# q and k of the first mixer in one pass over the feature blocks of a decoder layer, v behind them

## The chip, the cores and the metric

One core of a Trainium2 chip runs one decoder layer with float32 inputs. The metric is the device time of one execution in microseconds, as the median of three runs. TensorE (PE) multiplies, VectorE (DVE) and ScalarE (ACT) work on elements, GpSimd (POOL) takes a few subtractions and powers, and SyncE (SP) issues transfers.

## The reference

x is (1, 512, 1024), c is (1, 1024). All of it is computed in float32.

```python
mod = silu(c) @ ada_w + ada_b
shift1, scale1, gate1, shift2, scale2, gate2 = split(mod, 6)
h = rmsnorm(x, norm1_g) * (1 + scale1) + shift1
qa, ka, va, qb, kb, vb, ga, gb = split(h @ w_in)      # 512, 128, 128, 3 x 512, 2 x 1024 columns
ya = swa_attention(qa, ka, va, sinks, rel_bias) @ w_branch_a     # 8 q heads, 2 kv heads, window 128
yb = moba_attention(qb, kb, vb, rel_bias) @ w_branch_b           # 8 heads, blocks of 256
x = x + gate1 * ((sigmoid(ga) * ya + sigmoid(gb) * yb) @ w_out)
h2 = rmsnorm(x, norm2_g) * (1 + scale2) + shift2
x = x + gate2 * (square(relu(h2 @ w_mlp_in)) @ w_mlp_out)
return rmsnorm(x, final_g)
```

## The kernel before

The 512 tokens are four tiles of 128, the 1024 features are eight blocks of 128. Each float32 factor of a product is split in a rounded part (ScalarE, `split` line 71) and the rest (VectorE, line 72), and each product is issued three times (`mm3`, lines 76 to 78): high by high, high by low, low by high.

The change touches the first stage, from the loads to the start of the attention heads. It needs, for each block f of features, the columns shift1 and 1 + scale1. `ada_first` (line 266) loads the modulation weights of a block, 8 x 256 columns, blocks 0 and 1 together and the others singly. `columns` multiplies each of the eight row groups by silu(c) and adds them up, the first on ScalarE (line 292), seven on VectorE (line 294), in a PSUM bank that each group has for itself (`pac`); the last sum goes to SBUF (`acc`). TensorE then adds over the partitions with a column of ones (line 299), and `finish_cols` adds bias and 1 and multiplies by the gain in three small VectorE steps (lines 168 to 170). `normed` takes the mean square of a token tile on ScalarE (line 122), its power -1/2 on GpSimd (line 126) and scales x (line 309). `features` transposes block f of the scaled tiles to `px` (line 313), `modulated` scales and shifts it (line 317) and splits it to `hT` (lines 71 and 72), and `project` multiplies it with the 512 q columns of `w_in` into four banks `g0p` that stay open over all eight blocks: 4 x 3 products for a block. `g0_split` splits the q weights (ScalarE line 281, GpSimd line 282). Block 0 is done in two halves of two tiles.

Behind the loop k and v of the first mixer are multiplied from one load `kvr`: 24 products each, of 512 columns (`pkv`). `stack_q` and `stack_k` split the results and copy them to the other half of the partitions; all four q pairs are emitted ahead of the heads. Then `run` emits 16 heads, each with scores, softmax, transposes and values, and between them pieces of dense products as the table `PACE` says. The first dense pieces are `proj_v` (`pv`).

What sets the order: the program is written out in one order and a planner orders each engine's queue by a simulation. Within the first stage the queues of TensorE and SyncE follow the written order (`manual_schedule`), with later products put in between where the planner sees room; the other engines follow the planner. A tile of a pool waits for the buffer that it takes over, and PSUM has eight banks, all from one pool. SyncE has eight transfers under way at most: each issue takes over the semaphore of an older one.

Of the kernel before, what the change touches and what calls it, by code (L numbers as in the profile page):

```python
# [15 lines left out]
P = 128  # L16
# [21 lines left out]
def decoder_layer(ctx: ExitStack, tc: tile.TileContext, x, c, ada_w, ada_b, norm1_g, norm2_g, w_in,  # L38
# [63 lines left out]
    for g in range(2):  # L102
        V.tensor_scalar(swap[g], ident, 0.0, None, op0=ALU.mult)
        A.activation(swap[g][:, 64 * g:64 * g + 64], ident[:, 64 - 64 * g:128 - 64 * g], AF.Copy)
# [105 lines left out]
    with ExitStack() as sa:  # L210
# [30 lines left out]
        with ExitStack() as ss:  # L241
# [10 lines left out]
            n_ada = 0  # L252

            def ada_first(fs):

                nonlocal n_ada
                w, tiles, nk = len(fs) * P, [], KT // len(fs)
                for i in range(len(fs)):
                    name, n_ada = f"ad{n_ada}", n_ada + 1
                    n = n_ada - 1  # L260
                    t = (p0.tile([P, 2048], F32, name=name, tag=("at0h", "at0l", "at1h", "at1l")[n % 7])
                         if n % 7 < 4 else raw(name))
                    t = t.rearrange("p (k s n) -> p k s n", k=nk, s=2)
                    for s in range(2):
                        c0 = s * D + fs[0] * P
                        SY.dma_start(t[:, :, s], wk[:, i * nk:(i + 1) * nk, c0:c0 + w])
                    tiles.append(t)
                ads[fs[0]] = lambda k: tiles[k // nk][:, k % nk]

            def g0_load(k, n):  # L270
                if k % 2 == 0:
                    g0r[k] = pq.tile([P, 2, 512], F32, name=f"g0r{k}", tag="g0r", bufs=4)
                SY.dma_start(g0r[k // 2 * 2][:, k % 2:k % 2 + n], w0[:, k:k + n, 0:512])

            def g0_split(k):
                wr = g0r[k // 2 * 2][:, k % 2]
                wh = pq.tile([P, 512], F32R, name=f"g0h{k}", tag="g0h", bufs=2)
                wl = pq.tile([P, 512], F32R, name=f"g0l{k}", tag="g0l", bufs=2)
                perm = lambda t: t.rearrange("p (j g d) -> p j g d", j=4, g=2)
                src = wr.rearrange("p (g j d) -> p j g d", j=4, g=2)  # L280
                A.activation(perm(wh), src, AF.Copy)  # L281
                G.tensor_tensor(perm(wl), src, perm(wh).bitcast(F32), op=ALU.subtract)  # L282
                return wh, wl

            def columns(fs):

                w = len(fs) * P
                ad, pac = ads[fs[0]], bank(f"pac{fs[0]}")
                acc = p0.tile([P, 512], F32, name=f"acc{fs[0]}", tag="sh", bufs=2)
                acc = acc[:, 0:2 * w].rearrange("p (s n) -> p s n", s=2)  # L290
                part_ = pac[:, 0:2 * w].rearrange("p (s n) -> p s n", s=2)
                A.activation(part_, ad(0), AF.Copy, scale=cs[:, 0:1])  # L292
                for k in range(1, KT):
                    V.scalar_tensor_tensor(part_ if k < KT - 1 else acc, ad(k), cs[:, k:k + 1], part_,  # L294
                                           op0=ALU.mult, op1=ALU.add)
                yield
                for i, f in enumerate(fs):
                    for s in range(2):
                        nc.tensor.matmul(pac[:, 2 * i + s:2 * i + s + 1], acc[:, s, i * P:(i + 1) * P], ones_f[:, 0:1],
                                         start=True, stop=True)  # L300
                for i, f in enumerate(fs):
                    ab[f] = pqs.tile([P, 2], F32, name=f"ab{f}", tag="ab", bufs=4)
                    finish_cols(f, 0, 48, pac[:, 2 * i:2 * i + 2], ab[f])
                yield

            def normed(t):
# [8 lines left out]
            def modulated(f, px, t0, t1):  # L315
                cc = slice(t0 * P, t1 * P)
                A.activation(px[:, cc], px[:, cc], AF.Identity, bias=ab[f][:, 0:1], scale=ab[f][:, 1:2])
                split(hT[0][:, f, cc], hT[1][:, f, cc], px[:, cc])

            def project(f, t0, t1):  # L320
                cc = slice(t0 * P, t1 * P)
                for i in range(4):
# [4 lines left out]
            ads, g0r, ab, wgt = {}, {}, {}, {}  # L327
            sm = ss.enter_context(ExitStack())
            sm.enter_context(tc.manual_schedule(engines={mybir.EngineType.PE, mybir.EngineType.SP}))
            SY.dma_start(crow, c.rearrange("o (k p) -> (o k) p", p=P))  # L330
            SY.dma_start(rbx[0:32], rel_bias)
            SY.dma_start(oh, onehot)
            ada_first(GROUPS[0])
            SY.dma_start(stack[0:48], ada_b.rearrange("o (k p) -> (o k) p", p=P))
            SY.dma_start(stack[48:56], norm1_g.rearrange("o (k p) -> (o k) p", p=P))
            SY.dma_start(stack[56:64], norm2_g.rearrange("o (k p) -> (o k) p", p=P))
            for t in range(NT):
                SY.dma_start(x_sb[:, t, :], xr[:, t, :])
                if t == 1:
                    g0_load(0, 1)  # L340
            g0_load(1, 1)
            for i, fs in enumerate(GROUPS):
                if i:
                    if fs[0] % 2 == 0:
                        g0_load(fs[0], 2)
                    ada_first(fs)
            SY.dma_start(sink, attn_sinks.to_broadcast([P, NH]))

            cond(crow)
            cols_ = [columns(fs) for fs in GROUPS]  # L350
            next(cols_[0])

            for s in range(2):
                cc = slice(s * 512, (s + 1) * 512)
                prv, rv = bank(f"prv{s}"), scratch(f"rv{s}")
                nc.tensor.matmul(prv[:16], rbx, oh[:, cc], start=True, stop=True)
                V.tensor_copy(rv[:16], prv[:16, ::-1])
                SY.dma_start(rvd[:, 512 - s * 512:1024 - s * 512], rv[:16])
            rows(stack)
            next(cols_[0])  # L360
            px = bank("px0")
            g0p = [bank(f"g0p{i}") for i in range(4)]
            wgt[0] = g0_split(0)
            starts = {fs[0]: i for i, fs in enumerate(GROUPS)}
            for half in range(2):
                t0, t1 = 2 * half, 2 * half + 2
# [557 lines left out]
```

## Time and profile before

| | |
|---|---|
| median of three runs | 747.43 us (745.55 to 747.73) |
| profiled execution, its own time | 745.23 us |
| span of the profile | 743.5 us |
| TensorE busy | 709.7 us (95%) |
| VectorE, ScalarE, GpSimd busy | 459.1 us (62%), 344.6 us (46%), 28.7 us (4%) |
| transfers | 100.21 MB, mean 135 GB/s |

A busy TensorE is not a full one: matmuls are pipelined, and a row's duration contains the drain. How dense they are is read from the distance of two starts. A row of a timeline gives the start in us from the span's start, the duration, the engine, the line of the kernel, the operation, its tiles (out<-in), its shape and how often it came; in brackets stands the idle time of the engine ahead of it and what ended that. In the table of windows the busy times stand in the order TensorE, weight load, VectorE, ScalarE, GpSimd; behind them the granted clock as a share, the share of the 16 DMA engines and GB/s. "SPq" is an issue on SyncE's queue.

### The profile page before, as it was taken

How to read it: one execution, taken by the hardware profiler on the slowest of the kernel's cores; microseconds unless marked ns; L12 is line 12 of the kernel's file. 1: busy time of each engine (PE TensorE's matmuls, PEld its weight loads, DVE VectorE, ACT ScalarE, POOL GpSimd, SP SyncE). 2: the span in 40 equal slices, each digit the busy share in tenths (PEclk: the TensorE clock that was granted, in tenths of full speed). 3: DMA queues.
4: the chain of work that ended last, by engine and by line, in shares of the span. 5: the costliest groups of instructions: out<-in, count | busy, mean ns of one | idle time of the engine just before them, and what ended most of it. 6: DMA issues, size and time to landing. Idle time of an engine off the chain costs nothing.

```text
span 743.5 us, 9326 instructions
## 1 busy us (share of the span) xinstructions
PE 709.7 (95%) x3458; PEld 595.6 (80%) x3458; DVE 459.1 (62%) x959; ACT 344.6 (46%) x639; POOL 28.7 (4%) x40
## 2 busy tenths in 40 slices
PE   2799999998999999999999999999999999999996
PEld 1677889886887888888889888888888888888885
DVE  4874888887677867684478573252652527325765
ACT  3454787766786753343274442231332314322434
POOL 2220000000000000000120000000000000000001
PEclk9999999999999999999999999999999999999999
DMA  8994451566363864641415352233322332315103
GB/s 300 303 286 104 111 156 38 157 180 190 95 162 100 266 217 169 199 171 56 142 57 167 116 170 94 76 114 114 113 91 80 87 108 90 113 60 167 57 1 113
DMA packets 91146, 100.21 MB, mean 135 GB/s; under 512 B 3027, under 2 KB 70683, under 8 KB 91100
## 3 DMA queue, kind: packets, MB, share of 16 engines
q1 hardware_dynamic: 91100, 99.61, 43.6%
q8 instruction: 27, 0.44, 0.3%
q14 instruction: 19, 0.16, 0.1%
HBM read 94.03 MB, written 2.16 MB: 129 GB/s over the span
## 4 chain that ended last, share of the span: by engine, by line
PE 84%; ACT 4%; DMA 4%; DVE 3%; SPq 2%; issue 1%; POOL 0%; POOLq 0%; ACTq 0%; DVEq 0%
PE ph L77 8%; PE ph L76 8%; PE ph L78 8%; PE mo L78 7%; PE mo L76 7%; PE mo L77 7%; PE pg L76 3%; PE pg L78 3%; PE pg L77 3%; PE pqk L76 2%; PE py L78 2%; PE pqk L77 2%; PE py L76 2%; PE pqk L78 2%; PE py L77 2%
## 5 line engine op out<-in xcount | busy, mean ns | idle before, releaser
L800 ACT ACTIVATE r<-ph 128x512 f32<-128x512 f32 x32 | 18.8, 587 | 41.5 <-PE ph L78 26.8
L803 DVE TENSOR_TENSOR r<-r 128x512 f32<-128x512 f32 x32 | 21.9, 689 | 18.2 <-ACT a1h L802 8.0
L156 DVE SCALAR_TENSOR_TENSOR ac<-a,cs,ac 128x256 f32<-128x256 f32 x56 | 26.8, 479 | 3.5 <-ACT ac L154 2.9
L294 DVE SCALAR_TENSOR_TENSOR pac<-ad,cs,pac 128x256 f32<-128x256 f32 (+1 forms) x42 | 21.5, 523 | 9.8 <-ACT pac L292 9.4
L126 POOL TENSOR_TENSOR rstd<-rstd,mhalf 128x1 f32<-128x1 f32 x12 | 7.3, 610 | 373.3 <-DVE rstd L125 373.3
L711 DVE TENSOR_TENSOR rs<-mo,g2row 128x512 f32<-128x512 f32 x24 | 16.0, 686 | 9.1 <-PE mo L78 9.1
L445 ACT ACTIVATE pb<-pb,nb 128x128 f32<-128x128 f32 (+3 forms) x32 | 17.8, 557 | 8.1 <-DVE nb L444 7.7
L186 DVE SCALAR_TENSOR_TENSOR ma<-mw,cs,ma 128x512 f32<-128x512 f32 x28 | 21.0, 750 | 0.5
L76 PE MATMUL g0p<-hTh,g0h 128*128 128x512 f32 (+1 forms) x36 | 16.1, 448 | 3.8 <-ACT hTh L71 3.8
L445 ACT ACTIVATE pa<-pa,na 128x256 f32<-128x256 f32 (+1 forms) x32 | 15.2, 478 | 2.5 <-DVE na L444 2.4
L712 DVE TENSOR_TENSOR x_sb<-x_sb,rs 128x512 f32<-128x512 f32 x24 | 16.2, 685 | 0.0
L441 DVE CUSTOM_DVE_ANT_0 pa<-sa,ts,sink 128x256 f32<-128x256 f32 (+1 forms) x32 | 13.3, 445 | 3.8 <-PE sa L440 3.7
L441 DVE CUSTOM_DVE_ANT_0 pb<-sb,tm 128x128 f32<-128x128 f32 (+3 forms) x32 | 15.1, 488 | 0.2 <-PE sb L440 0.2
L77 PE MATMUL g0p<-hTl,g0h 128*128 128x512 f32 (+1 forms) x36 | 14.6, 406 | 0.0
L78 PE MATMUL g0p<-hTh,g0l 128*128 128x512 f32 (+1 forms) x36 | 14.4, 399 | 0.0
L440 PE MATMUL sb<-qk,qk 128*128 128x128 f32 (+3 forms) x64 | 12.8, 330 | 0.0
L76 PEld LDWEIGHTS g0p<-hTh,g0h 128*128 128x128 f32 x36 | 8.0, 222 | 5.1 <-ACT hTh L71 4.5
L282 POOL TENSOR_TENSOR g0l<-g0r,g0h 128x512 fp32r<-128x512 f32 x8 | 10.5, 1317 | 28.7 <-ACT g0h L281 24.4
L712 POOL TENSOR_TENSOR x_sb<-x_sb,rs 128x512 f32<-128x512 f32 x4 | 5.0, 1290 | 157.1 <-DVE rs L711 157.1
L440 PE MATMUL sa<-ka,qa 128*128 128x256 f32 (+1 forms) x64 | 10.9, 282 | 0.0
L470 PE MATMUL tb<-ident,pb 128*128 128x128 f32 x80 | 10.6, 274 | 0.3 <-DVE mb L441 0.3
L841 DVE TENSOR_TENSOR ml<-ml,g2row 128x512 f32<-128x512 f32 x8 | 5.1, 688 | 9.4 <-DMA ml<-in_w_mlp_out_dram 9.4
(1599 smaller groups left out, 2415.2 us busy)
## 6 DMA issues: line engine op xcount, KB each, us to landing
mi<-in_w_mlp_in_dram SPq DMA_DIRECT2D x16, 1024.0 KB, 6.3
mo<-in_w_mlp_out_dram SPq DMA_DIRECT2D x14, 1024.0 KB, 5.1
ad<-in_ada_w_dram SPq DMA_DIRECT2D x16, 512.0 KB, 7.9
a<-in_ada_w_dram SPq DMA_DIRECT2D x16, 512.0 KB, 5.3
gr<-in_w_in_dram SPq DMA_DIRECT2D x8, 1024.0 KB, 6.4
mw<-in_ada_w_dram SPq DMA_DIRECT2D x8, 1024.0 KB, 5.3
x_sb<-in_x_dram SPq DMA_DIRECT2D x8, 512.0 KB, 7.4
qkr<-in_w_in_dram SPq DMA_DIRECT2D x4, 1024.0 KB, 5.9
```

Of the source, the lines that this page charges most:

```text
L76: nc.tensor.matmul(o, w[0], m[0], start=first, stop=False, **kw)
L77: nc.tensor.matmul(o, w[0], m[1], start=False, stop=False, **kw)
L78: nc.tensor.matmul(o, w[1], m[0], start=False, stop=last, **kw)
L156: V.scalar_tensor_tensor(acc, ad[:, k], cs[:, k:k + 1], acc, op0=ALU.mult, op1=ALU.add)
L186: V.scalar_tensor_tensor(acc, t[:, k], c1, acc, op0=ALU.mult, op1=ALU.add)
L294: V.scalar_tensor_tensor(part_ if k < KT - 1 else acc, ad(k), cs[:, k:k + 1], part_, op0=ALU.mult, op1=ALU.add)
L440: nc.tensor.matmul(pb[:, :w], q[g][:, i * P:e], k[n][g][:, e - w:e], start=n == 0, stop=n == 1)
L441: V.tensor_tensor_reduce(p[:, o:o + w], pb[:, :w], b[:, w - 1::-1] if w < b.shape[1] else b[:, ::-1], scale=SCALE, scalar=-3e38 if sk is N ...
L445: A.activation(p[:, o:o + w], p[:, o:o + w], AF.Exp, bias=neg[:, i:i + 1], accum_out=sums[:, i:i + 1])
L712: add.tensor_tensor(x_sb[:, t, cc], x_sb[:, t, cc], tm, op=ALU.add)
L800: A.activation(r, ph, AF.Relu)
L803: V.tensor_mul(r, r, r)
```

## The change

- The loop multiplies q and k: `w_in`'s first 640 columns are loaded (`W_FIRST`) a block at a time, `project` works on five banks, k's (number 4) first, and k is ready with q. The weights of v are loaded alone and v is multiplied behind the loop.
- Every block's modulation weights are loaded singly, in two halves of four row groups, with the block's q and k weights between them. x tiles 0 and 1 come first on SyncE's queue; the table of the bias, the bias rows and the gains go to ScalarE's queue.
- The running sums of all blocks use one PSUM bank (`pa_`), the column sums another (`pm`). `sums` is cut in three pieces that are written between the other steps of VectorE.
- `beat(n)` issues n products of 240 columns of ones by ones into unused columns of `pm`: 12 behind the first transpose, 18 ahead of column sum 0, 8, 6, 6 and 10 later, all before block 1.
- In this stage all five engines follow the written order. In the loop, column sum f + 1 is written ahead of block f's products, and the transposes of f + 1 behind two fifths of them.
- `finish_cols` has two steps, since 1 is added to the bias once. The copies of `swap` go to VectorE.
- q pairs 1 to 3 are split after heads 0 to 2 are emitted (`next_q`), and `PACE` moves a dense piece from head 4 to head 1.

```diff
-GROUPS = ((0, 1), (2,), (3,), (4,), (5,), (6,), (7,))
-
-PACE = ((1, 1, 0), (0, 1, 0), (1, 1, 0), (1, 1, 0), (2, 1, 0), (0, 1, 0), (1, 1, 0), (1, 1, 0),
+W_FIRST = 640
+
+PACE = ((1, 1, 0), (1, 1, 0), (1, 1, 0), (1, 1, 0), (1, 1, 0), (0, 1, 0), (1, 1, 0), (1, 1, 0),
         (1, 2, 1), (1, 2, 1), (1, 2, 1), (1, 2, 1), (1, 2, 1), (1, 1, 2), (1, 0, 1), (1, 2, 1))
...
+        for s0 in (0, 3):
+            b = cols[:, (s0 + 1) * KT:(s0 + 2) * KT]
+            V.tensor_scalar(b, b, 1.0, None, op0=ALU.add)
...
-        V.tensor_scalar(ab[:, 1:2], pm[:, 1:2], bcol[:, b0 + KT:b0 + KT + 1], 1.0, op0=ALU.add, op1=ALU.add)
-        V.tensor_mul(ab[:, 1:2], ab[:, 1:2], cols[:, gain + f:gain + f + 1])
+        V.scalar_tensor_tensor(ab[:, 1:2], pm[:, 1:2], bcol[:, b0 + KT:b0 + KT + 1], cols[:, gain + f:gain + f + 1],
+                               op0=ALU.add, op1=ALU.mult)
...
+            def ada_first(f, half):
+                if half == 0:
+                    t = raw(f"ad{f}") if 4 <= f < 7 else p0.tile(
+                        [P, 2048], F32, name=f"ad{f}", tag=("at0h", "at0l", "at1h", "at1l")[f % 7])
+                    ads[f] = t.rearrange("p (k s n) -> p k s n", k=KT, s=2)
+                kk = slice(4 * half, 4 * half + 4)
+                for s in range(2):
+                    SY.dma_start(ads[f][:, kk, s], wk[:, kk, s * D + f * P:s * D + (f + 1) * P])
+            def g0_load(k):
+                g0r[k] = (pq.tile([P, W_FIRST], F32, name=f"g0r{k}", tag="g0r", bufs=4) if k < KT - 1 else
+                          p0.tile([P, W_FIRST], F32, name=f"g0r{k}", tag="br"))
+                SY.dma_start(g0r[k], w0[:, k, 0:W_FIRST])
             def g0_split(k):
+                wr = g0r[k]
+                wh = pq.tile([P, W_FIRST], F32R, name=f"g0h{k}", tag="g0h", bufs=2)
+                wl = pq.tile([P, W_FIRST], F32R, name=f"g0l{k}", tag="g0l", bufs=2)
+                perm = lambda t: t[:, :512].rearrange("p (j g d) -> p j g d", j=4, g=2)
+                src = wr[:, :512].rearrange("p (g j d) -> p j g d", j=4, g=2)
+                for h, l, r in ((wh[:, 512:], wl[:, 512:], wr[:, 512:]), (perm(wh), perm(wl), src)):
+                    A.activation(h, r, AF.Copy)
+                    G.tensor_tensor(l, r, h.bitcast(F32), op=ALU.subtract)
+                wgt[k] = wh, wl
+            def sums(f, k0, k1):
+                part_ = pa_[:, 0:256].rearrange("p (s n) -> p s n", s=2)
+                for k in range(k0, k1):
+                    if k == 0:
+                        A.activation(part_, ads[f][:, k], AF.Copy, scale=cs[:, k:k + 1])
+                        continue
+                    if k == KT - 1:
+                        acc[f] = p0.tile([P, 512], F32, name=f"acc{f}", tag="sh", bufs=2)[:, 0:2 * P].rearrange(
+                            "p (s n) -> p s n", s=2)
+                    V.scalar_tensor_tensor(acc[f] if k == KT - 1 else part_, ads[f][:, k], cs[:, k:k + 1], part_,
                                            op0=ALU.mult, op1=ALU.add)
+            def col_sums(f):
+                for s in range(2):
+                    nc.tensor.matmul(pm[:, 2 * f + s:2 * f + s + 1], acc[f][:, s], ones_f[:, 0:1], start=False, stop=True,
+                                     skip_group_check=True)
+            def columns(f):
+                ab[f] = pqs.tile([P, 2], F32, name=f"ab{f}", tag="ab", bufs=4)
+                finish_cols(f, 0, 48, pm[:, 2 * f:2 * f + 2], ab[f])
+            def gain_of(t):
                 square(xn[t], x_sb[:, t, :], ssq[:, t:t + 1])
                 rms(rstd[:, t:t + 1], ssq[:, t:t + 1], 0.0)
+            def normed(t):
                 V.tensor_scalar(xn[t], x_sb[:, t, :], rstd[:, t:t + 1], None, op0=ALU.mult)
...
+            def modulated(f, px, t0, t1, between=lambda: None):
                 cc = slice(t0 * P, t1 * P)
                 A.activation(px[:, cc], px[:, cc], AF.Identity, bias=ab[f][:, 0:1], scale=ab[f][:, 1:2])
...
+                A.activation(hT[0][:, f, cc], px[:, cc], AF.Copy)
+                between()
+                V.tensor_tensor(hT[1][:, f, cc], px[:, cc], hT[0][:, f, cc].bitcast(F32), op=ALU.subtract)
             def project(f, t0, t1):
                 cc = slice(t0 * P, t1 * P)
...
+                for i in (4, 0, 1, 2, 3):
                     mm3(g0p[i][:, cc], at(wgt[f], slice(None), slice(i * P, (i + 1) * P)),
                         at(hT, slice(None), f, cc), first=f == 0 and t0 == 0, last=f == KT - 1, skip_group_check=True)
                     yield
...
+            def beat(n, first=False):
+                for i in range(n):
+                    nc.tensor.matmul(pm[:, 16:256], ones_r, ones_r[:, 0:1].to_broadcast([P, 240]),
+                                     start=first and i == 0, stop=True, skip_group_check=True)
+            ads, g0r, ab, wgt, acc = {}, {}, {}, {}, {}
             sm = ss.enter_context(ExitStack())
...
+            sm.enter_context(tc.manual_schedule(engines={
+                mybir.EngineType.PE, mybir.EngineType.SP, mybir.EngineType.DVE, mybir.EngineType.Activation,
+                mybir.EngineType.Pool}))
+            A.dma_start(rbx[0:32], rel_bias)
+            A.dma_start(oh, onehot)
+            A.dma_start(stack[0:48], ada_b.rearrange("o (k p) -> (o k) p", p=P))
+            A.dma_start(stack[48:56], norm1_g.rearrange("o (k p) -> (o k) p", p=P))
+            A.dma_start(stack[56:64], norm2_g.rearrange("o (k p) -> (o k) p", p=P))
             SY.dma_start(crow, c.rearrange("o (k p) -> (o k) p", p=P))
...
+            for t in range(2):
                 SY.dma_start(x_sb[:, t, :], xr[:, t, :])
...
+            for f in range(KT):
+                ada_first(f, 0)
+                g0_load(f)
+                ada_first(f, 1)
+                if f == 0:
+                    for t in range(2, NT):
+                        SY.dma_start(x_sb[:, t, :], xr[:, t, :])
+            cond(crow)
+            prv, rv = [bank(f"prv{s}") for s in range(2)], [scratch(f"rv{s}") for s in range(2)]
+            px, pm, pa_ = bank("px0"), bank("pm"), bank("pa")
+            g0p = {i: bank(f"g0p{i}") for i in (4, 0)}
+            beat(12, True)
+            for t in range(2):
+                gain_of(t)
+                normed(t)
+            for s in range(2):
+                nc.tensor.matmul(prv[s][:16], rbx, oh[:, s * 512:(s + 1) * 512], start=True, stop=True)
+                V.tensor_copy(rv[s][:16], prv[s][:16, ::-1])
+                SY.dma_start(rvd[:, 512 - s * 512:1024 - s * 512], rv[s][:16])
             SY.dma_start(sink, attn_sinks.to_broadcast([P, NH]))
...
+            features(0, px, 0, 2)
             rows(stack)
...
+            g0p.update({i: bank(f"g0p{i}") for i in (1, 2, 3)})
+            g0_split(0)
+            sums(0, 0, KT)
+            beat(18)
+            col_sums(0)
+            gain_of(2)
+            normed(2)
+            columns(0)
+            gain_of(3)
+            beat(8)
+            modulated(0, px, 0, 2, lambda: normed(3))
+            for _ in project(0, 0, 2):
+                pass
+            features(0, px, 2, NT)
+            beat(6)
+            modulated(0, px, 2, NT)
+            sums(1, 0, KT)
+            g0_split(1)
             for f in range(KT):
+                if 0 < f < KT - 1:
+                    col_sums(f + 1)
                 for i, _ in enumerate(project(f, 2 if f == 0 else 0, NT)):
...
+                    if f + 1 < KT and i == (0 if f == 0 else 1):
                         px = bank(f"px{f + 1}")
                         features(f + 1, px, 0, NT)
...
+                    if f + 1 < KT and i == (4 if f == 0 else 3):
+                        if f == 0:
+                            beat(6)
+                            col_sums(1)
+                            beat(10)
+                        if f + 2 < KT:
+                            sums(f + 2, 0, 3)
+                        columns(f + 1)
+                        modulated(f + 1, px, 0, NT, lambda: f + 2 < KT and sums(f + 2, 3, 6))
+                        if f + 2 < KT:
+                            sums(f + 2, 6, KT)
+                            g0_split(f + 2)
             sm.close()
...
+            ka = [slot(n, f"ka{n}", F32R) for n in (4, 5, 6, 7)]
+            ka = stack_k("ka", g0p[4], ka[:2], ka[2:])
+            qa = []
+            def next_q():
+                j = len(qa)
+                if j < 4:
+                    qa.append(stack_q(f"qa{j}", g0p[j], [qk_tile(f"qa{j}{g}") for g in range(2)]))
+            next_q()
+            vr = raw("vr")[:, 0:KT * P].rearrange("p (k n) -> p k n", k=KT)
+            SY.dma_start(vr, w0[:, :, C_VA:C_VA + P])
+            w = wide("vaw")
+            split(w[0], w[1], vr)
+            pva_ = bank("pvaf")
+            for k in range(KT):
+                mm3(pva_, at(w, slice(None), k), at(hT, slice(None), k), first=k == 0, last=k == KT - 1)
             vaf = scratch("vaf")
...
+            A.activation(vaf, pva_, AF.Copy)
...
-            return Head(f"a{h}", qa[j], ka, g, lambda kb: va[:, kb, 2 * g:2 * g + 2].rearrange("p c d -> p (c d)"), attnT[0], j,
+            head = Head(f"a{h}", qa[j], ka, g, lambda kb: va[:, kb, 2 * g:2 * g + 2].rearrange("p c d -> p (c d)"), attnT[0], j,
                         [(0, 128), (128, 256), (384, 256), (640, 256)],
                         [[(0, (0, 1)), (1, (1, 2))], [(2, (2, 3)), (3, (3,))]], (256, 256, 256, 128),
                         toeplitz(h, 1, 256, "ts"), sink[:, h:h + 1])
+            next_q()
+            return head
```

## Rows read from the trace of the kernel before

**Rows 1.** Windows by stage, all engines: window, busy us and instructions, clock, DMA, GB/s.

```profile
0.00:22.66 22.66, 6.80 (x17) 2.85 (x17) 11.06 (x30) 9.07 (x17) 6.93 (x14) 1.00 0.92 300
...
31.98:72.84 40.86, 38.07 (x193) 31.22 (x193) 26.56 (x64) 20.19 (x33) 7.78 (x6) 1.00 0.79 214
...
170.00:190.00 20.00, 16.31 (x75) 13.23 (x74) 12.57 (x34) 11.61 (x23) 0.52 (x1) 0.91 0.60 158
```

**Rows 2.** What TensorE waited for, whole span: us in total, times, longest.

```profile
PE pac L299 <- DVE acc L294: 5.4, 2, 3.9
...
PE ob L488 <- ACT cb L484: 2.0, 1, 2.0
PE ob L481 <- ACT ptb40h L71: 1.7, 1, 1.7
...
PE ta L470 <- DVE pa L456: 1.2, 1, 1.2
```

**Rows 3.** Timeline of TensorE: start, us, operation, count, wait before it.

```profile
22.66 0.58 PE L76 MATMUL g0p<-hTh,g0h 128*128 128x256 f32 x1 [2.75 <-ACT hTh L71]
...
27.76 0.58 PE L77 MATMUL g0p<-hTl,g0h 128*128 128x256 f32 x1
...
31.77 0.42 PE L78 MATMUL g0p<-hTh,g0l 128*128 128x256 f32 x1
31.98 0.61 PE L76 MATMUL g0p<-hTh,g0h 128*128 128x512 f32 x1
...
36.32 0.40 PE L78 MATMUL g0p<-hTh,g0l 128*128 128x512 f32 x1
36.55 0.60 PE L313 MATMUL px<-ident,xn 128*128 128x128 f32 x4
...
58.21 0.28 PE L76 MATMUL pv<-vw00h,hTh 128*128 128x256 f32 x1
...
60.00 0.28 PE L76 MATMUL pv<-vw01h,hTh 128*128 128x256 f32 x1
...
72.62 0.39 PE L78 MATMUL pkv<-hTh,kvw1l 128*128 128x512 f32 x1
```

**Rows 4.** Timeline of the start, other engines and SyncE's queue.

```profile
0.72 1.28 ACT L137 ACT_TABLE_LOAD   x1 [0.72 <-PEq L910]
...
4.93 0.96 SPq L335 DMA_DIRECT2D stack<-in_norm_g_dram  x1
...
11.65 0.67 DVE L357 COPY rv<-prv 16x512 f32<-16x512 f32 x1
...
13.81 1.06 ACT L122 ACTIVATE xn<-x_sb 128x1024 f32<-128x1024 f32 x1 [3.65 <-DMA x_sb<-in_x_dram]
...
15.07 1.06 ACT L122 ACTIVATE xn<-x_sb 128x1024 f32<-128x1024 f32 x1
15.23 0.56 POOL L126 TENSOR_TENSOR rstd<-rstd,mhalf 128x1 f32<-128x1 f32 x1 [12.82 <-DVE rstd L125]
15.82 0.75 DVE L309 TENSOR_SCALAR xn<-x_sb,rstd 128x1024 f32<-128x1024 f32 x1
...
26.30 0.54 ACT L317 ACTIVATE px<-px,ab 128x256 f32<-128x256 f32 x1 [1.97 <-PE px L313]
```

**Rows 5.** Timeline of the block loop, VectorE and ScalarE.

```profile
33.46 1.53 DVE L294 SCALAR_TENSOR_TENSOR pac<-ad,cs,pac 128x256 f32<-128x256 f32 x3
...
35.55 0.21 DVE L168 TENSOR_SCALAR ab<-pac,cols 128x1 f32<-128x1 f32 x1
...
38.62 0.68 DVE L72 TENSOR_TENSOR hTl<-px,hTh 128x512 fp32r<-128x512 f32 x1
...
36.42 0.46 ACT L292 ACTIVATE pac<-ad,cs 128x256 f32<-128x256 f32 x1
37.19 0.75 ACT L317 ACTIVATE px<-px,ab 128x512 f32<-128x512 f32 x1 [0.31 <-PE px L313]
37.97 0.60 ACT L71 ACTIVATE hTh<-px 128x512 fp32r<-128x512 f32 x1
```

More of the change, by code (lines that the diff above doesn't have):

```diff
@@ L103, in decoder_layer @@
         V.tensor_scalar(swap[g], ident, 0.0, None, op0=ALU.mult)
-        A.activation(swap[g][:, 64 * g:64 * g + 64], ident[:, 64 - 64 * g:128 - 64 * g], AF.Copy)
+        V.tensor_copy(swap[g][:, 64 * g:64 * g + 64], ident[:, 64 - 64 * g:128 - 64 * g])
     mhalf = pz.tile([P, 1], F32, name="mhalf")
@@ L250, in decoder_layer @@
             V.memset(rbx, 1.0)
[L252 to L273, printed above, removed]
-            def g0_split(k):
[L276 to L294, printed above, removed]
-                                           op0=ALU.mult, op1=ALU.add)
[L296 to L304, printed above, removed]
@@ L349, in decoder_layer @@
[L349 to L358, printed above, removed]
-            rows(stack)
-            next(cols_[0])
@@ L361, in decoder_layer @@
[L361 to L366, printed above, removed]
-                for t in range(t0, t1):
-                    normed(t)
-                features(0, px, t0, t1)
-                modulated(0, px, t0, t1)
-                if half == 0:
-                    for _ in project(0, 0, 2):
-                        pass
@@ L376, in decoder_layer @@
+            features(0, px, 2, NT)
[3 more added lines that the diff above has]
+            g0_split(1)
             for f in range(KT):
+                if 0 < f < KT - 1:
+                    col_sums(f + 1)
                 for i, _ in enumerate(project(f, 2 if f == 0 else 0, NT)):
-                    if i == 0 and f + 1 < KT:
+                    if f + 1 < KT and i == (0 if f == 0 else 1):
                         px = bank(f"px{f + 1}")
                         features(f + 1, px, 0, NT)
-                        modulated(f + 1, px, 0, NT)
@@ L382, in decoder_layer @@
-                    if i == 2 and f + 2 in starts:
-                        n = starts[f + 2]
-                        advance(cols_[n])
-                        if n + 1 < len(GROUPS):
-                            advance(cols_[n + 1])
-                if f + 2 < KT:
-                    wgt[f + 2] = g0_split(f + 2)
-            sm.close()
-            kvr = raw("kvr").rearrange("p (k n) -> p k n", k=KT)
-            SY.dma_start(kvr, w0[:, :, C_KA:C_KA + 2 * P])
-            pkv = []
-            for s in range(2):
-                w = wide(f"kvw{s}")
-                split(w[0], w[1], kvr[:, :, s * P:(s + 1) * P])
-                pkv.append(bank(f"pkv{s}"))
-                for k in range(KT):
-                    mm3(pkv[s], at(w, slice(None), k), at(hT, slice(None), k), first=k == 0, last=k == KT - 1)
-                if s == 0:
-                    qa = [stack_q("qa0", g0p[0], [qk_tile(f"qa0{g}") for g in range(2)])]
-                    ka = [slot(n, f"ka{n}", F32R) for n in (4, 5, 6, 7)]
-                    ka = stack_k("ka", pkv[0], ka[:2], ka[2:])
+                    if f + 1 < KT and i == (4 if f == 0 else 3):
[10 more added lines that the diff above has]
+                            g0_split(f + 2)
@@ L404, in decoder_layer @@
+            w = wide("vaw")
[3 more added lines that the diff above has]
+                mm3(pva_, at(w, slice(None), k), at(hT, slice(None), k), first=k == 0, last=k == KT - 1)
             vaf = scratch("vaf")
-            A.activation(vaf, pkv[1], AF.Copy)
-            qa += [stack_q(f"qa{j}", g0p[j], [qk_tile(f"qa{j}{g}") for g in range(2)]) for j in range(1, 4)]
+            A.activation(vaf, pva_, AF.Copy)
         def turn_v():
```

23 lines of the change are left out of this document (removed).

## The prediction, made before the changed kernel ran

> **What bounds the kernel now.** I read windows by stage first, then what TensorE waits for, then the timelines of the first 73 us. TensorE idles 15.86 of the first 22.66 us, 2.79 of the 40.86 to 72.84 and 3.69 of the 20 from 170 on [rows 1]; gaps are all that a change which keeps the products can win, and most stand ahead of the first product, at 22.66 us [rows 3]. The longest waits after the start are for the first column sums, for head 0's probabilities (1.2 us, "ta" on "pa") and, in the head stage, for "cb" and "ptb40h" (2.0 and 1.7 us) [rows 2]. The first products run at half rate: 256 columns are 0.21 us apart at 31.77 us (1.2 GHz), while 512 columns are 0.23 us apart at 36.32 us (2.4 GHz) [rows 3]; the granted clock of the windows does not tell the two apart here, the spacing does. What I compare is the moment at which TensorE has finished q, k and v of the first mixer. Before, the last v product starts at 72.62 and its successor would start at 72.84; between 58.21 and 60.12 us 16 products of the next stage ("pv") had slipped in, 1.9 us [rows 3]. So the like moment is 70.9 us, and everything behind it is the same list of products.
>
> **The change, part by part.** The products stay: k moves from 24 products behind the loop into it (15 instead of 12 per block), v stays behind it. 60 products on constants ("beats") are new, all ahead of block 1. The three-step finish of a block's columns becomes two steps.
>
> *The start.* Five loads go to ScalarE's queue ahead of its table load. The same kind of issue took SyncE up to 0.96 us and the table load 1.28 us [rows 4]; five of 0.4 to 1.0 us from 0.7 us on, then the load, make ScalarE free at 4.0 to 7.0, and I take 5.1. The two x tiles go first in SyncE's queue. Then: two squares, each 1.26 us to the next [rows 4], to 7.8; sum step and hand-overs 0.4, power 0.56 and scaling 0.75 of tile 1 [rows 4], to 9.5; two copies of 0.67 and three small operations on VectorE [rows 4], to 11.4. The seven running sums of block 0 form a chain on VectorE: three took 1.53 us with 0.48 for the last, so 0.52 each [rows 5]; 3.65 for seven, to 15.0. Behind them in VectorE's fixed order stand tile 2's sum step, power and scaling (1.5) and the two finishing steps (0.36, estimated from 0.21 for one before [rows 5]), to 16.9. From the modulation of two tiles to the product that needs its last part it was 1.46 us before (26.30 to 27.76) [rows 3, 4]; tile 3's scaling stands in VectorE's way for 0.5 of it, so the second product of block 0 is at 18.8, its first near 18, against 22.66 before. 14 products of 256 columns at full rate take 1.6, two transposes 0.3, the second half's modulation 1.46: 22.2. Block 1's seven sums, only now in VectorE's order: 3.65, to 25.9. Block 2 shares its PSUM tile with block 1, so its first sum (ScalarE, 0.46) must wait for block 1's last; with two more on VectorE, to 27.4. The ten beats issued behind column sum 1 end at 27.3 at full rate and hide there. Finish 0.36, modulation 0.78 + 0.65, low part 0.65, two more sums 1.0 [rows 5]: block 2's sums are complete at 31.0 us. Ends: 30.0 with a fast ScalarE queue, 33.5 if TensorE is still at half rate (below).
>
> *The loop.* Column sum f+1 now stands ahead of block f's products on TensorE; behind it queue all 15 products and the next transposes. That closes a ring: last sum of f+1 done, hand-over 0.05; two column sums 0.4 (an estimate from the four transposes that end 0.60 after their start [rows 3]); six products of 0.23, 1.38; four transposes 0.60; modulation 0.78, rounding 0.65, low part 0.65, two sums 1.0, hand-over 0.05 [rows 3, 5]. Together 5.56 us a block. TensorE has 0.4 + 15 x 0.23 + 0.36 = 4.2 us of work in it and waits 1.35. VectorE and ScalarE alone, on the one shared tile, need 7 x 0.52 + 0.36 + 0.65 + 0.5 = 5.2, so 5.2 to 5.7 bounds it. Before, each block had a bank of its own, and the whole stretch to 72.84 idled 2.79 us [rows 1]; five turns of the ring idle 6.75. The last sums are done at 31.0 + 5 x 5.56 = 58.8; block 6 takes 4.2, block 7 waits 0.3 for its low part and takes 3.45, to 66.8; v's 24 products 5.5, to 72.3. Behind a waiting first sum on ScalarE stand the next block's modulation and weight split, both counted in the ring. The stream of x, modulation and q/k weights grows by 0.5 MB to 13.1 MB (sizes from the code): at the first 22.66 us' 300 GB/s [rows 1] it ends near 46 us, and the last block's first sums are due at about 53, so it costs nothing; a ring below 4.5 us a block would meet it. The weights of v are hidden: they land long before, and their split (one rounding, one subtraction) fits between the last transposes at 61.3 and 66.8; without that cover it would cost about 1 us, as the k weights did before.
>
> *Behind it.* Head 0's k and its first q tile come out of the loop's end, some 5 us before v is done; before they came after k's own stage. I take the 1.2 us wait of "ta" on "pa" [rows 2] as gone; it can also stay, or grow by as much again, because three q results now hold PSUM banks until heads 0 to 2 are out. The q tiles 1 to 3 move behind the heads, with the same 12 roundings, subtractions and copies through SyncE's queue. The other waits of the head stage I leave as they are.
>
> *Sum.* 72.3 - 70.9 = +1.4; -1.2; +0.2 us. The profiled execution took 745.23, 2.2 below the median of the three runs (747.43), so I add to the median: 747.6.
>
> **The rivals.** 0.3%, 2.2 us, is about what a measurement of this kernel tells from no change.
>
> A, faster: the head stage gains. Its two large waits are for ScalarE (2.0 + 1.7 = 3.7 [rows 2]), and k and q are ready some 5 us earlier, with fewer q splits ahead of the heads, so that ScalarE and VectorE run ahead of TensorE. If both go, 0.2 - 3.7 = -3.5, 743.9; with the rest of the 3.69 us that TensorE idles between 170 and 190 us [rows 1], some 742. For it: TensorE alone is near its limit there, so these waits come from the order of the queues. Against it: they lie 100 us later, and a new order makes new ones.
>
> B, slower: the beats do not lift the rate before block 0. Place: block 0's first half. At half rate 14 products take 3.0 instead of 1.6, transposes 0.2 more, and the ten beats 2.0 instead of 1.0, which then outlast the sums of block 2 by 0.8: 2.4 in all, block 2's sums at 33.4, time 750.0. It decides as soon as block 2's sums are later than about 33.0. For it: before, products ran from 22.66 us on and the rate rose only after 31.98 [rows 3]; the beats leave gaps of 0.5 and 1.4 us around the column sum. Against: 18 beats of 0.2 us are 3.6 us in a row, where before TensorE had idled 2.75 us ahead of the first product [rows 3].
>
> The Trainium skill bears on the last 0.8 of B: PSUM — Partial Sum Buffer, "PSUM bank collisions raise a hardware error", has engines kept apart by bank and quadrant and not by address, so that the finish of block 1, which reads other columns of the bank that the beats write, waits for all ten. No row of this trace shows such a pair; without the rule B would be 749.2.
>
> C, the clock falls inside the loop: 1.35 us idle in every 5.56. Fifteen products at half rate take 6.9 instead of 3.45, the ring 7 to 8: +10 us, 758. The mean clock is 0.91 in the stretch 170 to 190 us, around the wait of 2.0, and 1.00 between 31.98 and 72.84 us [rows 1], which holds a wait of 1.5 (5.4 less 3.9 [rows 2]); so it is unlikely.
>
> D, the change does not do what it says: the compiler's order lets v's or later products into the loop's gaps as it did with "pv". Up to 6.75 us of gaps would fill, 741. All eight banks are taken in the loop, so there is nowhere to put them.
>
> **How the numbers follow.** My forecast 0.37; A 0.32; B and like delays of the start, as a late x tile, 0.24; C 0.03; D 0.03; 0.01 left to others on the slow side. A and D are the faster side, 0.35, B and C the slower, 0.28. The likeliest alone spans 745.3 to 749.6 (start 30.0 to 33, ring 5.2 to 5.7, partly against each other). A reaches down to 742, D to 741, B up to 750.0 and, with the longer ring, 751. With the edges of A and B held and D and C left out: 742.0 to 751.5.
>
> **What would show it.** First product of block 0 near 18 us, and 0.11 to 0.12 us between its 256-column products (0.21 is B). Block 1 at 31 to 32 us, then blocks 5.2 to 5.7 us apart, with one TensorE wait of about 1.3 us on "acc" in each. Blocks closer than 5 us would break my ring and give 2 to 3 us back. The last v product at 71 to 74 us; the waits on "pa", "cb" and "ptb" in the head stage decide between A and my forecast. I am wrong if the moment comes before 69 us or if the head stage moves by more than 3 us either way.

## The result and the profile after

The changed kernel takes 751.03 us (median of five runs, 750.45 to 751.77); the kernel before takes 747.43 (745.55 to 747.89, five runs beside it). The ratio is 1.0055, 95% interval 1.0038 to 1.0071: slower by 3.6 us. The profiled execution of the changed kernel took 751.15 us, its span is 749.2. The profiled execution before stands 2.2 us under its own median, this one 0.1 over it, so between the two profiles there are 5.9 us to explain, of which 3.6 are the change's in the medians. Single executions of one kernel differ with the granted clock: of 76 of the kernel before, timed beside the runs below, the nine with a mean clock of 0.996 or 0.997 took 744.9 us on average, the thirteen with 0.987 to 0.990 took 750.1.

Windows of the changed kernel: the first, the second with the third, and the fourth answer to [rows 1] (its second row goes from 31.98 to 72.84 us in one); behind them stand block 1's turn, the turn after it and the head stage's first part:

```profile
0.00:22.66 22.66, 17.73 (x74) 13.32 (x74) 10.57 (x32) 9.16 (x18) 5.66 (x14) 0.92 1.00 297
31.98:40.86 8.88, 8.38 (x30) 6.72 (x31) 4.65 (x12) 2.98 (x6) 1.71 (x3) 0.68 1.14 311
40.86:72.84 31.98, 27.85 (x146) 22.43 (x145) 21.00 (x46) 14.54 (x25) 7.31 (x9) 1.00 0.56 163
170.00:190.00 20.00, 16.79 (x85) 13.67 (x84) 16.86 (x43) 12.30 (x25) 0.52 (x1) 0.95 0.57 156
...
31.96:37.50 5.54, 5.54 (x17) 4.66 (x18) 2.54 (x7) 1.29 (x3) 0.37 (x1) 0.50 1.12 315
37.50:43.00 5.50, 5.00 (x25) 3.85 (x25) 4.11 (x10) 2.42 (x5) 1.74 (x2) 0.99 1.15 313
...
76.00:105.00 29.00, 27.29 (x169) 24.44 (x168) 22.11 (x73) 20.10 (x52) 1.04 (x2) 0.94 0.53 139
```

The start is fuller (17.73 us busy, 9.6 of it beats), the stretch from 31.98 to 72.84 us idles 0.50 + 4.13 = 4.63 us where it idled 2.79, and one stretch stands out: from 31.96 to 37.50 us the granted clock is 0.50, which is 1.2 GHz. TensorE's waits, answering to [rows 2]:

```profile
PE pm L297 <- DVE acc L292: 8.7, 7, 3.5
...
PE ob L512 <- ACT cb L508: 1.8, 1, 1.8
PE oa L505 <- ACT pta00h L71: 1.2, 1, 1.2
...
PE oa L505 <- DVE pta00l L72: 0.5, 1, 0.5
```

The wait of "ta" on "pa" is gone, and so is that on "ptb40h"; "oa" on "pta00" is new. TensorE's timeline, answering to [rows 3]:

```profile
18.22 0.43 PE L76 MATMUL g0p<-hTh,g0h 128*128 128x256 f32 x1
...
20.20 0.41 PE L78 MATMUL g0p<-hTh,g0l 128*128 128x256 f32 x1
20.41 0.35 PE L76 MATMUL g0p<-hTh,g0h 128*128 128x256 f32 x1
20.60 0.28 PE L77 MATMUL g0p<-hTl,g0h 128*128 128x256 f32 x1
20.72 0.28 PE L78 MATMUL g0p<-hTh,g0l 128*128 128x256 f32 x1
...
27.12 1.35 PE L333 MATMUL pm<-ones_r 128*128 128x240 f32 x10
31.96 1.01 PE L297 MATMUL pm<-ones_r,acc 128*128 128x1 f32 x4 [3.49 <-DVE acc L292]
...
33.84 0.63 PE L78 MATMUL g0p<-hTh,g0l 128*128 128x512 f32 x1
34.26 0.63 PE L76 MATMUL g0p<-hTh,g0h 128*128 128x512 f32 x1
...
45.36 0.61 PE L297 MATMUL pm<-ones_r,acc 128*128 128x1 f32 x4 [1.04 <-DVE acc L292]
```

Three things are to be seen. Block 0's products begin at half rate (0.21 us apart) and pass to full rate at about 20.5. Then TensorE idles 3.49 us ahead of column sum 2, and block 1's products stand 0.43 us apart, half rate again. From block 3 on a turn has one wait of 1.02 to 1.04 us.

The start and the loop on the other engines, answering to [rows 4, 5]; the last two rows are of a later turn:

```profile
2.82 0.36 ACTq L345 DMA_DIRECT2D stack<-in_norm_g_dram  x1
3.20 1.28 ACT L137 ACT_TABLE_LOAD   x1 [3.20 <-DVE swap L104]
...
28.51 0.22 DVE L171 SCALAR_TENSOR_TENSOR ab<-pm,cols 128x1 f32<-128x1 f32 x1 [0.35 <-PE pm L333]
...
31.43 0.48 DVE L292 SCALAR_TENSOR_TENSOR acc<-ad,cs,pa 128x256 f32<-128x256 f32 x1
...
45.86 1.01 DVE L292 SCALAR_TENSOR_TENSOR pa<-ad,cs,pa 128x256 f32<-128x256 f32 x2 [0.55 <-ACT pa L287]
...
49.36 0.69 DVE L321 TENSOR_TENSOR hTl<-px,hTh 128x512 fp32r<-128x512 f32 x1 [0.85 <-ACT hTh L319]
```

The last sums ("acc") of blocks 0 to 7 end at 14.99, 26.60, 31.91, 39.66, 45.31, 50.96, 56.61 and 62.26 us: after block 2 one turn of 7.75, then four of 5.65.

v's last product starts at 77.53 and is followed at 77.76; 18 "pv" products of 0.12 us stand ahead of that, so the moment of the prediction is 75.6, against 70.9 before. From there to the first product of the last stage ("ph") it was 314.4 us before and is 315.7 now; behind it 358.1 and 357.9. So the 5.7 us between the two spans are 4.7 of the first stage, 1.3 of the head stage, and -0.2.

Not all of the 1.3 need be the change's. The window from 150 to 200 us before, in the changed kernel and in run 8 below, which has the old first stage:

```profile
150.00:200.00 50.00, 46.31 (x227) 38.74 (x226) 35.59 (x102) 32.52 (x62) 1.56 (x3) 0.97 0.57 159
150.00:200.00 50.00, 46.60 (x228) 38.70 (x227) 36.81 (x100) 32.25 (x62) 1.56 (x3) 0.93 0.61 168
150.00:200.00 50.00, 46.22 (x222) 38.54 (x221) 34.43 (x98) 32.26 (x61) 1.56 (x3) 0.93 0.56 157
```

All three have a wait of 1.8 to 2.0 us on "cb" in it, and half rate follows; in the profiled execution before it took less, by 0.04 of 50 us, about 2 us. Run 4, without the change's head part, has 0.93 here too, and run 3, with both parts, 0.97: it follows no part of the change, and one trace of each kernel can't say more.

### The profile page after: what moved, and what is told of

Read it like the earlier page. It is cut to its first block, busy times and chain, and to the rows that moved or that the text cites. A ratio compares the mean times of both kernels' runs of the same rounds, so it can differ in the third digit from the quotient of the medians.

```text
span 749.2 us, 9490 instructions
## 1 busy us (share of the span) xinstructions
PE 723.2 (97%) x3521; PEld 606.7 (81%) x3521; DVE 460.6 (61%) x953; ACT 345.3 (46%) x645; POOL 31.8 (4%) x48
## 4 chain that ended last, share of the span: by engine, by line
PE 81%; DVE 8%; ACT 4%; DMA 3%; issue 2%; SPq 1%; POOLq 0%; POOL 0%; ACTq 0%; DVEq 0%
PE ph L77 8%; PE ph L78 8%; PE ph L76 8%; PE mo L76 7%; PE mo L77 7%; PE mo L78 7%; PE pg L76 4%; PE pg L77 4%; PE pg L78 4%; PE py L78 2%; PE py L77 2%; PE py L76 2%; DMA ad<-in_ada_w_dram 2%; PE ob L505 1%; PE wo L76 1%
## 5 line engine op out<-in xcount | busy, mean ns | idle before, releaser
L292 DVE SCALAR_TENSOR_TENSOR pa<-ad,cs,pa 128x256 f32<-128x256 f32 x48 | 23.4, 487 | 4.3 <-ACT pa L287 3.4
L76 PE MATMUL g0p<-hTh,g0h 128*128 128x512 f32 (+1 forms) x45 | 19.1, 424 | 0.4 <-ACT hTh L319 0.4
L77 PE MATMUL g0p<-hTl,g0h 128*128 128x512 f32 (+1 forms) x45 | 17.9, 398 | 0.1
L78 PE MATMUL g0p<-hTh,g0l 128*128 128x512 f32 (+1 forms) x45 | 17.6, 391 | 0.0
L318 ACT ACTIVATE px<-px,ab 128x512 f32<-128x512 f32 (+1 forms) x9 | 6.3, 701 | 20.3 <-PE px L314 16.5
L279 POOL TENSOR_TENSOR g0l<-g0r,g0h 128x128 fp32r<-128x128 f32 (+1 forms) x16 | 13.9, 866 | 35.1 <-ACT g0h L278 34.6
L297 PEld LDWEIGHTS pm<-ones_r,acc 128*128 128x128 f32 x32 | 4.6, 206 | 12.4 <-DVE acc L292 12.4
L297 PE MATMUL pm<-ones_r,acc 128*128 128x1 f32 x32 | 5.3, 268 | 9.7 <-DVE acc L292 8.7
L333 PE MATMUL pm<-ones_r 128*128 128x240 f32 x60 | 11.7, 366 | 1.1 <-DVE rstd L125 1.1
L321 DVE TENSOR_TENSOR hTl<-px,hTh 128x512 fp32r<-128x512 f32 (+1 forms) x9 | 5.7, 631 | 10.5 <-ACT hTh L319 10.4
```

What stands on the lines that cost most here:

```text
L76: nc.tensor.matmul(o, w[0], m[0], start=first, stop=False, **kw)
L77: nc.tensor.matmul(o, w[0], m[1], start=False, stop=False, **kw)
L78: nc.tensor.matmul(o, w[1], m[0], start=False, stop=last, **kw)
L292: V.scalar_tensor_tensor(acc[f] if k == KT - 1 else part_, ads[f][:, k], cs[:, k:k + 1], part_, op0=ALU.mult, op1=ALU.add)
```

## The experiments

Eleven runs, each kernel timed in five rounds beside the kernel before, whose median was 747.0 to 747.2 us in all of them, with single executions from 744.1 to 753.5. A difference to the changed kernel is one of medians. "Stretch" is the time from v's end to the first "ph" product in the profiled execution: one execution, which the scatter of the runs moves by 2 to 3 us. All edits are on the changed kernel unless it is said.

**1. Beats in the gap ahead of block 1.**

```diff
                         columns(f + 1)
+                        if f == 0:
+                            beat(26)
```

> 26 more beats stand behind the finish of block 1, so that TensorE works through most of the 3.49 us that it idled ahead of block 1. Theory (block 1 runs at half rate because of that idle stretch, and its turn of the ring takes 7.75 instead of 5.65 us): block 1's 512-column products 0.23 us apart from the first one on, turn 5.65 us, v's moment 2.1 us earlier, time about 749.0. Rival (block 1's turn is long because its sums or loads are late, the rate is a symptom): turn stays near 7.7 us, time 751.

Measured 748.29 us (746.82 to 749.97), ratio to before 1.0012 (1.0000 to 1.0025), 2.7 less than the changed kernel. TensorE's timeline of this kernel:

```profile
29.11 3.16 PE L333 MATMUL pm<-ones_r 128*128 128x240 f32 x26 [0.38 <-DVE ab L173]
32.23 0.61 PE L297 MATMUL pm<-ones_r,acc 128*128 128x1 f32 x4
32.69 0.48 PE L76 MATMUL g0p<-hTh,g0h 128*128 128x512 f32 x1
33.01 0.39 PE L77 MATMUL g0p<-hTl,g0h 128*128 128x512 f32 x1
33.24 0.39 PE L78 MATMUL g0p<-hTh,g0l 128*128 128x512 f32 x1
```

The products of block 1 stand 0.23 us apart where they stood 0.43, although they start as late; the sums of block 3 follow those of block 2 by 5.64 instead of 7.75. Nothing else is changed, so the idle gap is what took the rate away, and it cost 2.1 us of turn. Where the gap stays unfilled, the same turn takes 7.74 or 7.75 us in all profiles with this loop, the changed kernel's and those of runs 2, 4, 5 and 6. v ends 1.8 us earlier, at 73.8, since the start was 0.3 later; the rest of the 2.7 lies in the stretch (314.3), where the first head's values wait as in the changed kernel (1.2 and 0.5 us), but the clock from 75 to 105 us is 1.00.

**2. One beat instead of 60.**

```diff
-                for i in range(n):
+                for i in range(1 if first else 0):
```

> Only the first of the 60 beats is left (it opens the bank). Theory (as placed, the beats bring block 0's second part to full rate and nothing more, and the ten ahead of block 1's finish cost 0.35): block 0 at half rate throughout, block 2's sums done at 32 to 33 us instead of 31.9, block 1 at half rate as in the changed kernel; time 751.3 to 752.5. Rival (the beats carry the start): block 2's sums later than 34 us and half rate into block 2, time 754 or more.

Measured 751.91 us (750.16 to 752.47), 1.0051 (1.0035 to 1.0068). Inside the theory's range. All of block 0's first half ran 0.21 us apart, block 2's sums were done at 32.73 and the moment came at 76.4, 0.8 us later. The beats as they were placed are worth about a microsecond: in the changed kernel's profile the rate rose behind ten of the first 15 products, and it was lost again before block 1.

**3. The column sum behind the transposes.**

```diff
-                if 0 < f < KT - 1:
-                    col_sums(f + 1)
...
                         features(f + 1, px, 0, NT)
+                        if 0 < f < KT - 1:
+                            col_sums(f + 1)
```

> Column sum f+1 stands behind the transposes of f+1 instead of ahead of block f's products. Theory (the ring through the column sum sets the pace of 5.65 us a block): first product of block 1 near 30.4 us, blocks 5.1 to 5.2 us apart by VectorE's sums and ScalarE's first sum, v's moment 3.7 us earlier if block 1 is still at half rate and 5.3 if not, time 747.3 or 745.7. Rival (VectorE's chain of sums sets the pace wherever the column sum stands): blocks 5.6 us apart, only the 1.5 us of block 1's earlier start, time 749.5.

Measured 744.36 us (741.58 to 745.62), 0.9950 (0.9931 to 0.9970): 6.7 us less than the changed kernel and faster than before, by more than the theory said. The rival falls: the turns are 5.63 for the first, then 5.09 and three of 4.86 or 4.87; v ends at 70.5 instead of 75.6, though block 1's first product comes at 31.39 and not at 30.4. The stretch is 313.8, 1.9 us less, which the theory did not have. TensorE of this kernel around block 1, then VectorE in the loop of the kernel of run 9, which has this edit:

```profile
28.18 1.35 PE L333 MATMUL pm<-ones_r 128*128 128x240 f32 x10
31.39 0.49 PE L76 MATMUL g0p<-hTh,g0h 128*128 128x512 f32 x1 [1.85 <-ACT hTh L319]
...
32.91 0.39 PE L77 MATMUL g0p<-hTl,g0h 128*128 128x512 f32 x1
33.14 0.53 PE L78 MATMUL g0p<-hTh,g0l 128*128 128x512 f32 x1
...
36.03 0.63 PE L78 MATMUL g0p<-hTh,g0l 128*128 128x512 f32 x1
36.46 0.50 PE L76 MATMUL g0p<-hTh,g0h 128*128 128x512 f32 x1
36.79 0.39 PE L77 MATMUL g0p<-hTl,g0h 128*128 128x512 f32 x1
```

```profile
44.04 1.01 DVE L292 SCALAR_TENSOR_TENSOR pa<-ad,cs,pa 128x256 f32<-128x256 f32 x2 [0.55 <-ACT pa L287]
...
46.75 0.69 DVE L321 TENSOR_TENSOR hTl<-px,hTh 128x512 fp32r<-128x512 f32 x1
47.36 0.48 DVE L292 SCALAR_TENSOR_TENSOR pa<-ad,cs,pa 128x256 f32<-128x256 f32 x1
```

The gap is 1.85 instead of 3.49 us, and only a few products run at half rate, from 33.46 us on. In the loop VectorE no longer waits 0.85 us for the rounding ahead of the low part; what it still waits for is the first sum on ScalarE, 0.55 a turn. TensorE waits 0.2.

**4 to 6. The head part: both halves undone, then one at a time.** Run 4 has the old PACE and q's pairs 1 to 3 split ahead of the heads, run 5 the old PACE alone, run 6 the split ahead alone.

```diff
-PACE = ((1, 1, 0), (1, 1, 0), (1, 1, 0), (1, 1, 0), (1, 1, 0), (0, 1, 0),
+PACE = ((1, 1, 0), (0, 1, 0), (1, 1, 0), (1, 1, 0), (2, 1, 0), (0, 1, 0),
...
             A.activation(vaf, pva_, AF.Copy)
+            for _ in range(3):
+                next_q()
```

> The head part is undone: the q pairs 1 to 3 are split ahead of the heads and PACE is that of the kernel before. Theory (the two waits of the first head's values on pta00, 1.2 and 0.5 us, come from the changed order of the heads): they go, the first head's wait on its probabilities may come back with 1.2; time 750 to 751. Rival (the head part saves what it was written for): waits between 80 and 130 us grow by more than 1.5 us, time 752.5 or more. First stage as in the changed kernel for both, block 2's sums at 31.9, turns of 5.65.

> The changed kernel (751.0 us) with the old list PACE, q's tiles 1 to 3 still split behind heads 0 to 2. The old head part whole won 4.3 us; which half holds that? Theory: the q splits standing between the heads hold ScalarE and VectorE up, and the list matters little: 749.5 to 751.5 here, the waits of oa on pta stay. Rival: the list sets where the first turns stand and holds the 4 us: 746 to 748, those waits gone.

> The changed kernel with q's tiles 1 to 3 split ahead of the heads, as before, and the new list PACE. Theory (the q splits hold the cost): 746 to 748, no wait of oa on pta. Rival (the list holds it): 749.5 to 751.5. If both halves give about 2 us, the two add; if neither gives anything, only both together do.

Measured: run 4 746.75 us (0.9988, 0.9976 to 0.9999), stretch 311.5; run 5 749.19 (1.0017, 1.0002 to 1.0032), stretch 312.6; run 6 748.06 (0.9999, 0.9979 to 1.0018), stretch 312.3. Run 4 misses both expectations: the head part costs 4.3 us, when I expected at most one. Run 5 lies between theory and rival, run 6 at the edge of its theory. The halves give 1.8 and 3.0 and nearly add up; the split between the heads looks the larger, but the intervals of runs 5 and 6 overlap. The waits of "oa" on "pta00" are gone in all three, also where only PACE is undone, which the theory of run 5 did not expect. The window 76 to 105 us, in run 4 and in run 6:

```profile
76.00:105.00 29.00, 29.00 (x191) 26.24 (x190) 23.90 (x75) 24.00 (x59) 1.16 (x2) 1.00 0.52 141
```

```profile
76.00:105.00 29.00, 28.79 (x187) 25.62 (x186) 22.99 (x74) 22.15 (x56) 1.05 (x2) 1.00 0.51 131
```

Against the changed kernel's row above, 27.29 at a clock of 0.94: it idles 1.7 us, and the 0.06 of 29 us that the lower rate took makes another 1.7. (Run 1 has the same idle time there and kept the rate, so the second part belongs to the execution.) Where it idles, ScalarE first and then TensorE of the changed kernel show:

```profile
95.48 1.04 ACT L71 ACTIVATE qkw10h<-qkr 128x1024 fp32r<-128x1024 f32 x1
96.43 0.57 ACT L71 ACTIVATE pta00h<-ta 128x512 fp32r<-128x512 f32 x1
...
97.06 0.39 PE L505 MATMUL oa<-pta00h,va 128*128 128x256 f32 x1 [1.23 <-ACT pta00h L71]
...
98.62 0.39 PE L505 MATMUL oa<-pta00l,va 128*128 128x256 f32 x1 [0.48 <-DVE pta00l L72]
...
99.72 0.63 PE L76 MATMUL pqk<-hTh,qkw01h 128*128 128x512 f32 x1
100.15 0.63 PE L77 MATMUL pqk<-hTl,qkw01h 128*128 128x512 f32 x1
```

Head 0's transposes come so late that the split of a later weight, 1.04 us, stands ahead of the split of its probabilities; "oa" waits, and the dense products behind it are 0.43 us apart. In runs 4 to 6 the probabilities' split stands first (at 95.43 in run 6, the weight's at 96.27) and the wait is gone. But it stands first in run 3 too, and there the wait remains with 0.9 us; so this order is not the whole cause, and an order with only these two exchanged was not tried.

**7. Three edits: run 3, run 4 and 14 beats in the gap.**

> Three edits on the changed kernel: the column sum behind the transposes (alone 6.7 us less), the old head part (alone 4.3 less), and 14 beats behind the finish of block 1 to hold the rate over the gap. Theory, the savings stand in different stages and add: 739.5 to 741.5 us, v's end some 5.5 us earlier than in the changed kernel and the head stage 311 to 312 us long. Rival, the head stage gives back what an earlier start brings, as it did for part of the gain in other runs: 743 to 745.

Measured 743.39 us (740.99 to 746.64), 0.9944 (0.9920 to 0.9967). At the median the savings do not add up to the theory's. v ends at 68.8, 6.8 earlier than in the changed kernel, but in the profiled execution (746.64, the slowest of its ten) the stretch is 318.2. Three of its waits of TensorE between 68 and 180 us:

```profile
PE pv L77 <- DVE vw02l L72: 1.5, 1, 1.5
PE ta L498 <- DVE pa L484: 1.3, 1, 1.3
PE ta L498 <- DVE ma L469: 1.3, 1, 1.3
```

The rate is a part of it too: the clock from 105 to 150 us is 0.96 and from 150 to 200 us 0.93, where run 3 has 1.00 and 0.97; that is some 3.8 of the 4.4 us by which the stretch is longer than run 3's. Five of the ten executions took 741.0 to 742.6 us at a mean clock of 0.994 to 0.997, close to the theory, the others 744.2 to 746.6 at 0.990 to 0.993; so how far the savings add stays open.

**8. The head part alone on the kernel before** (new PACE, q split behind heads 0 to 2).

> The kernel before (747.4 us) with the change's head part alone: the new list PACE, and q's tiles 1 to 3 split behind heads 0 to 2. Theory, the head part costs the same wherever k and q come from: 750 to 752. Rival, it costs only together with the earlier k and q, and on the kernel before it gains or is neutral: 746 to 748.5.

Measured 746.25 us (744.47 to 750.81), 0.9988 (0.9965 to 1.0012): no difference. The head part costs only together with the new first stage. The theory falls. (The profiled execution, 747.75 us, has a stretch of 316.2; it is 1.5 us above its own median, as that of the kernel before is 2.2 below.)

**9 to 11. Run 3 with the q split ahead (9), with the whole old head part (10), with 14 beats in the gap (11).**

> The column sum behind the transposes (alone 744.4 us) and q's tiles 1 to 3 split ahead of the heads (alone 3.0 less than the changed kernel); the new list PACE and no beats added. Theory, the head stage follows its own order and the savings of the two stages add: 740.5 to 742.5, the stretch from v's end to the last stage's first product 311 to 313 us. Rival, the head stage answers to the hour at which it starts, and an earlier start is given back there: 743.5 to 745, that stretch 313.5 or longer.

> As the kernel with all three edits (743.4 us), without its 14 beats behind the finish of block 1. Theory, the beats only hold the rate of the next few products, worth 0.5 to 1 us: 743.5 to 745. Rival, savings add and the three-edit kernel lost something by its beats: 740 to 742.

> The column sum behind the transposes (alone 744.4 us) with 14 beats behind the finish of block 1, the change's head part as it is. Theory, the beats save the half rate of block 1's first six products, 6 x 0.2 = 1.2 us at most, and v ends 1 us earlier; the head stage passes it on: 743 to 744. Rival, the head stage gives it back: 744 to 745.5.

Measured: run 9 742.54 us (740.67 to 743.54), 0.9921 (0.9892 to 0.9951); run 10 743.09 (0.9928, 0.9903 to 0.9953); run 11 743.59 (0.9949, 0.9928 to 0.9970). Stretches 312.0, 312.2 and 315.2. Run 9 lies at the edge of its theory, run 10 between theory and rival, run 11 inside its theory. Run 9's median is the lowest of all kernels, 0.8% under before, but its interval overlaps those of runs 3, 7, 10 and 11. The q split ahead gives 1.8 us here, inside the intervals; the old PACE and the beats give nothing that can be told from zero. Run 11's v ends 0.5 us earlier than run 3's (70.0), and its head stage has the 1.5 us wait on "vw02l" of run 7: in that execution the earlier start was given back, and more.

## Why the prediction was wrong

Forecast 747.6, measured 751.03, inside the range of 742.0 to 751.5; no difference was the forecast, and it is slower. Step by step:

- *Start, right in kind, 0.9 us short.* Table load at 3.20, ScalarE free at 4.5 (5.1 forecast), first product at 18.22 (near 18), block 2's sums at 31.91 (31.0); with the same first stage they came at 32.1 to 33.2 in runs 4 to 6. (The working has a slip: from 5.1 two squares of 1.26 end at 7.6, not at 7.8.) The 18 beats did not lift the rate before block 0 but behind ten of its first 15 products, so rival B's condition held for that part. The ten beats did not hide, though they ran at full rate (1.35 us): column sum 1 came 0.7 us later than forecast, they began at 27.12, and the finish of block 1 waited 0.35 us for them. By the Trainium skill's rule on banks (PSUM — Partial Sum Buffer, "PSUM bank collisions raise a hardware error") it was to wait for all ten, and the row at 28.51 agrees; whether the chip needs that wait or only the program makes it, no run shows.
- *The failed step: block 1 at full rate.* My own numbers left TensorE idle from 27.3 to 31.0, 3.7 us, and the rows before already showed half rate behind an idle of 2.75 us. I used that for block 0 and not for block 1, and rival C looked for idle time only inside the turns of the loop. There C was rightly unlikely: the waits of 1.04 us left the clock at 1.00. The gap ahead of them took the rate away for 5.5 us and cost 2.1 (run 1).
- *Ring, right.* 5.65 us a turn, 5.56 forecast, one wait on "acc" in each: 0.45 over five turns. What closes it is the place of the column sum, as the working had it (run 3: 4.86 to 5.09 with it moved). My bound of 5.2 from VectorE and ScalarE alone was too high, by 0.3 at least.
- *v's end.* 75.6 against 72.3: 0.9 + 2.1 + 0.45, and 0.15 less from the last sums to v's end. The last v product, due at 71 to 74, started at 77.53, with 2.2 us of "pv" ahead of it.
- *Head stage, -1.2 forecast, +1.3 between the two profiles.* The wait on "pa" did go. I left the rest as it was, and the change's own head part set a new wait of 1.7 us in its place; that part costs 4.3 us in the medians (run 4). Against that, earlier k and q bring something, as rival A said: without the head part the stretch is 2.9 us shorter than before (run 4: 311.5 against 314.4), and A had 3.7. But A had it from two waits, and only the one on "ptb40h" (1.7) is gone there; that on "cb" stays, with 1.9 us.
- *Sum.* The measured time is 3.4 us over the forecast, and the first stage alone, 0.9 + 2.1 + 0.45 - 0.15, is 3.3 of it. Between the profiles the head stage adds 2.5, and the profiled execution before, 2.2 us under the median to which I added, takes about as much back. The two can't be told apart with one trace each. In the medians, 3.6 us slower with 4.7 of it from the first stage and -0.2 at the end, the head stage would be about 0.9 shorter (an estimate from these numbers): near the forecast of -1.2, but by luck, since neither the 4.3 nor what stands against it was in the sum.

What stays open: why the head part is free on the old first stage and costs 4 us on the new one; and how much of each stretch is scatter of one execution, of its granted clock above all.

## What to carry to other kernels

Price every idle stretch of TensorE twice, once as a wait and once by the rate of the products behind it, and do so for the gaps that the new schedule itself makes. A small product whose input arrives late belongs behind the work that does not need it: ahead of that work it closes a ring through TensorE, ScalarE and VectorE. Time an edit of a later stage apart from one of an earlier: here one cost 4 us on one first stage and nothing on another. And before two single traces are subtracted, compare their granted clocks stage by stage.

## What was not expected of the hardware

The rate follows the gaps with a delay, down and up, and the delay differs between executions. In run 3 the products right behind an idle of 1.85 us stand 0.23 us apart, and those some 4 us later 0.43; in run 11, with 14 beats in that gap, the clock from 30 to 40 us is 1.00. In the changed kernel 18 beats and 8 more did not lift the rate, ten half-rate products later it rose; behind the same beats between 5 (run 7) and all 15 (runs 3, 9, 11) products of block 0's first half ran at half rate.

Shorter waits than the 3.49 us can cost rate as well: in every profile, before and after, one wait of 1.3 to 2.2 us on "cb", some 185 us into the span, goes with a fall to half rate, while the waits of 1.04 us in each turn of the loop leave the clock at 1.00.

Filling a gap of 3.49 us with 26 products on constants of 0.12 us each took 2.1 us out of block 1's turn, at no time of its own.
